# Residual and gate offsets by accumulating DMAs, and more Strassen pairs, in a float32 encoder block

## The chip, the cores and the metric

The kernel runs on one core of a Trainium2 chip. The metric is the device time of one execution in microseconds (us). The engines are TensorE (PE, with PEld for its weight loads and "PE mm" or "PE at" for its work into one or the other set of PSUM banks), VectorE (DVE), ScalarE (ACT), GpSimd (POOL) and SyncE (SP), whose queue starts the weight loads.

## The reference

One encoder layer with 256 tokens of width 2048, in float32:

```
h = LN(alpha*h + 0.5*SwiGLU_1(h))                  # hidden width 5504
h = LN(alpha*h + W_out[sig(g_A)*(A(h) W_oA) + sig(g_B)*(B(h) W_oB)])
h = LN(alpha*h + CrossAttn(h, LN(mem)))            # 4 heads, 256 memory tokens
h = LN(alpha*h + 0.5*SwiGLU_2(h))

swiglu_ffn(x, w_in, w_out): g, u = split(x @ w_in); return (silu(g) * u) @ w_out
g = sigmoid(gates + gate_bias); g_a, g_b = split(g, 2)
```

A is chunked attention with relative-position bias, B is latent attention with a low-rank key and value. The gates `gates` are 4096 columns of one combined projection of h.

## The kernel before

**Products.** All products keep float32 accuracy with operands of a shorter type: every operand is split into a part hi and a rest lo, and hi·hi, hi·lo and lo·hi are summed in PSUM. A weight block of 128 rows and 2048 columns (`raw`, 1 MB) comes by SP's queue; ScalarE casts it to `hi` in two halves (`halves`, L264) and VectorE subtracts to get `lo` (L267). Work goes by pairs of contraction tiles. A plain pair (`mm_pair`, matmuls at L311) has 24 matmuls of 128x512 for four results (two token halves by two column halves).

**Summed pairs.** A pair can also be done in the manner of Strassen (`mm_sums`, matmuls at L366) with 21 matmuls. For it VectorE adds blocks of the weights (`weight_sums`, L248 once on 1024 columns and L250 twice on 512), subtracts a lo of only 1536 columns, and the sums are split as well: ScalarE casts them to X2 in two halves, VectorE subtracts to X3 (L267, 2048 columns). X2 and X3 (`SUM_HOME`) are there once. The activations need a matching form (`forms_step`, `sum_forms`: L321 and four L325 on VectorE, a split by L255 on ScalarE and L256 on VectorE), which is kept at a home that the tables `SUMS_...` name. Of each summed pair part of the results goes to four further PSUM banks (`qs`), which `shared` (L676 on) combines at the end of a group: two copies on ScalarE, four additions on VectorE (L681 to L684). They are added to what the other pairs made in their own banks (`ps`).

**Groups.** `pair_group` (L640 on) lays out the pairs of a group of results in an order, and `at` says which are summed. There are eight pairs in a group of 16 contraction tiles. An FFN runs in two halves of its hidden width (24 and 19 tiles). Each has first its input groups of eight pairs, whose end is the gated product (L725 to L728), then its output. Half 0 has two output groups g0 and g1 of 12 pairs with pairs 3, 5, 7, 9 summed, in the order 0 to 11 (`out_pair`). Half 1 has one of 10 pairs with 3, 5 and 7 summed, and another kind of group (`out_proj`). At the end of `out_pair` the shared results are added to the residual h by VectorE, four operations on 128x512 with the factor ALPHA in the first half (L629) and without in the second (L631); then `finish` (L754) adds each token's and column half's own PSUM bank to h. The cross attention's output product `w_xo` uses `out_pair`, too.

**Gates.** Four groups n of 1024 columns (L917 to L927): `product` adds shared results and PSUM banks to H{n} (L921), adds the bias (L923), which four DMAs on POOL's queue have spread over the partitions of X1 (L912), and takes the sigmoid on ScalarE. Groups 0 and 1 have four summed pairs in the order `ORDER_GATE`, 2 and 3 have three. Then comes the group `w_lat`.

**Order.** `weave` puts steps between the pairs of a group by position; `add` gives a step a priority. Within that a scheduler orders each engine's instructions by times of its own, so a row may move where the code doesn't say so. Buffers: three `raw`, two `hi` and `lo`, six small tiles `w2` (shown as `w`), and in PSUM four banks `mm` and four `at`, between which groups alternate.

Of the kernel before, what the change touches and what calls it, by code (L numbers as in the profile page):

```python
# [14 lines left out]
ALU = mybir.AluOpType  # L15
# [3 lines left out]
P = 128  # L19
S = 256  # L20
D = 2048
KT = D // P
# [5 lines left out]
SUMS_IN = {2: ("X0", 0), 4: ("X0", 1), 6: None}  # L28
AT_FIRST = 4, 6
SUMS_OUT = ({3: ("X1", 0), 5: ("X1", 1), 7: ("X0", 0), 9: ("X0", 1)},  # L30
            {3: ("X1", 0), 5: ("X1", 1), 7: ("X0", 0)})
SUMS_GATE, AT_GATE = {**SUMS_IN, 5: ("F", 0)}, ((2, 4, 5, 6), (2, 4, 5, 6), (2, 4, 6), (2, 4, 6))
ORDER_GATE = (0, 2, 1, 4, 5, 3, 6, 7)
SUMS_YB = {4: ("T0", 0), 6: ("T0", 1), 2: None}
AT_YB = (2, 4, 6), (4, 6)
SUMS_XQ = {4: ("H5", 0), 6: ("H5", 1), 2: None}
# [5 lines left out]
SUM_HOME = ("X2", "X3"),  # L42
# [5 lines left out]
ALPHA = 2.0 ** 0.25  # L48
# [53 lines left out]
class Kernel:  # L102
# [451 lines left out]
    def ffn(self, tag, xT, st, first=None, steps=None, late=None, before=None, tags=None):  # L554


        t = self.t
        f0 = bank = 0
        turn = None
        fx = {}  # L560
        for half, nf in enumerate(F_SPLIT):
            hid, fh, homes = Act([]), {}, SUMS_OUT[half]
            end = half == len(F_SPLIT) - 1
            form = lambda c, fh=fh, homes=homes, hid=hid: self.forms_step(fh, homes, c, lambda: hid)
            for g in range(-(-nf // 4)):
# [12 lines left out]
                if turn and n < 4:  # L578
                    turn[5] = turn.pop(6)
                self.weave(main, turn or {}, prio=0)  # L580
                for c, (home, _) in homes.items():
                    if home == "X1" and c // 2 == g - 1:
                        self.add(form(c))
                hidden, turn = self.hidden(ps, bank, g, n, hid, qs)
                self.add(hidden, prio=SOON)
                if before and 2 <= j < 6:
                    self.add(lambda q=j - 2: self.gb_apply(2, self.h, (q,)), prio=LATE)
                if j == 0 and first is not None:
                    for c in set(SUMS_IN) - set(AT_FIRST):
                        self.add(self.forms_step(fx, SUMS_IN, c, xT, False))  # L590
                bank ^= 1
            if end and late:
                self.add(lambda: setattr(self, "cut", True))

            def out(hid=hid):
                x = lambda: hid
                src = [t[tag + "_w_out"][g, :, f0 * 1024:(f0 + nf) * 1024] for g in range(2)]
                self.out_pair(bank, src[0], 0, nf, x, homes, fh, half == 0, st if end else None,
                              SUM_HOME + ("H5",) if end else SUM_HOME)
                if end:  # L600
                    self.out_proj(tag + "_w_out_r", nf, x, False, st, steps, tags, 2, cut=tags is None)
# [17 lines left out]
    def out_pair(self, bank, src, g, nk, x, at, fx, scale, st, sums_in=SUM_HOME):  # L619

        nc, h = self.nc, self.h
        ps, qs = {}, {}

        def shared():
            for (tt, a), s in qs["add"].items():
                c = (2 * g + a) * 512
                hs = h[tt][:, c:c + 512]
                if scale:
                    nc.vector.scalar_tensor_tensor(hs, hs, ALPHA, s, ALU.mult, ALU.add)  # L629
                else:  # L630
                    nc.vector.tensor_tensor(hs, hs, s, ALU.add)  # L631
# [238 lines left out]
    def mixer(self, xT, st, steps):  # L870
        nc, t = self.nc, self.t
# [24 lines left out]
        ps = {}  # L896
# [3 lines left out]
        a, b, c = steps(1)  # L900
        self.weave(first, {0: a, 3: b, 4: c})
        gates, fx = {}, {}
# [4 lines left out]
        bias = {}  # L907

        def load_bias(n):
            if "t" not in bias:  # L910
                bias["t"] = self.block("X1", (P, 2, 1024))
            nc.gpsimd.dma_start(bias["t"][:, n % 2, :], t["gate_row"][n:n + 1, :].to_broadcast([P, 1024]))  # L912

        def gate(n):
            ps, qs = {}, {}

            def product():  # L917
                g = gates[n] = self.block(f"H{n}", (P, 2, 2, 512))
                for tt in range(2):
                    for a in range(2):  # L920
                        nc.vector.tensor_tensor(g[:, tt, a, :], qs["add"][tt, a], ps[tt, a], ALU.add)  # L921
                    v = g[:, tt].rearrange("p a n -> p (a n)")
                    nc.vector.tensor_tensor(v, v, bias["t"][:, n % 2, :], ALU.add)  # L923
                    nc.scalar.activation(v, v, AF.Sigmoid)
                if n < 2:
                    load_bias(n + 2)
            self.pair_group(n % 2, t["w_gate"][n], 512, KT, xT, AT_GATE[n], fx, ps, qs, None, SUM_HOME + ("H5",),  # L927
                            ORDER_GATE if len(AT_GATE[n]) > 3 else None)
# [54 lines left out]
        self.pair_group(0, t["w_lat"][0], 512, KT, xT, SUMS_IN, fx, lps, lqs, None, SUM_HOME + ("H5",))  # L983
        self.add(lat_scale, prio=SOON)
        self.add(lat_planes)

# [225 lines left out]
        for i in range(NA):  # L1212
            side = [[lat_send(0)], [], [lat_join(0)], [lat_join(1)]][2 * i:2 * i + 2] if i < 2 else ([], [])
# [42 lines left out]
        n = B_HEADS - 1  # L1256
# [55 lines left out]
        main = self.collect(lambda: out_a(0))  # L1312
# [4 lines left out]
        side = out_b(0)  # L1317
        last = {}
        main = self.collect(lambda: last.update(out_b(1)))
# [379 lines left out]
def _layout(i):  # L1699
    import numpy as np  # L1700
    a = {k: np.asarray(v) for k, v in i.items()}
    r = {}
# [5 lines left out]
    for f in ("ffn1", "ffn2"):  # L1708
        w = a[f + "_w_in"][0]
        r[f + "_w_in"] = _pairs(  # L1710
            w[:, D_FF:D_FF + NG * 512], w[:, :NG * 512], 512, [AT_FIRST] + [SUMS_IN] * (NG - 1))
        r[f + "_w_in_r"] = _pairs(
            w[:, D_FF + NG * 512:], w[:, NG * 512:D_FF], D_FF - NG * 512, [SUMS_IN])
        w = a[f + "_w_out"][0]
        at = [*SUMS_OUT[0], *(F_SPLIT[0] // 2 + c for c in SUMS_OUT[1])]
        r[f + "_w_out"] = _pairs(*_halves(w), 512, [at, at])
# [60 lines left out]
```

## Time and profile before

| | us |
|---|---|
| runs of the kernel before | 2432.69, 2434.71 (median), 2434.84 |
| the profiled execution | 2432.52 |
| its span | 2430.7 |
| ScalarE busy in it | 1553.2 (64%) |
| POOL busy in it | 35.9 (1%) |
| first FFN, output groups g0 and g1 | 256.63 to 319.19, to 381.9 |
| gate groups 0 to 3 | 729.85, 770.49, 812.16, 853.97, end 895.78 |
| second FFN, output groups g0 and g1 | 1995.23 to 2057.8, to 2120.5 |

The span is that of the profiler's records; the execution's own time lies 1.8 us above it. The granted TensorE clock was 1.00 throughout. In a timeline a row gives the start, the time taken and the line; VectorE's operations overlap a little at their ends, so that the distance between two starts is what one costs its engine. A table by windows gives each engine's busy time in a stretch.

### The profile page before, as it was taken

Reading aid. Unit: us, or ns where it says so; the run is one execution under the profiler, and the core shown is the slowest. Engines: PE = TensorE matmul, PEld = TensorE weight load, DVE = VectorE, ACT = ScalarE, POOL = GpSimd, SP = SyncE. Lnnn points to the kernel's source line nnn. Section 1 sums busy time; section 2 is a strip of 40 time slices with the busy share of each in tenths; the row PEclk is TensorE's granted clock in tenths of the full one; section 3 lists DMA queues with packets and bytes.
Section 4 is the critical chain, followed back from the end, with each engine's and each line's share of the span. In section 5 each row is a group of like instructions: output and inputs, shape, how many; then the busy total and the mean of one; then the engine's idle time right before and its main releaser. Section 6 shows DMA issues by size and latency. Waiting matters only on the chain.

```text
span 2430.7 us, 29702 instructions
## 1 busy us (share of the span) xinstructions
PE 2422.3 (100%) x11280; PEld 2022.8 (83%) x11280; DVE 2130.9 (88%) x2437; ACT 1553.2 (64%) x2022; POOL 35.9 (1%) x81
## 2 busy tenths in 40 slices
PE   9999999999999999999999999999999999999999
PEld 8888888888888888888888888888888888888887
DVE  8999989899889998779788889979879999888997
ACT  6676745666555557878565687765666675556662
POOL 0000000000000001000000000000000000000000
PEclk9999999999999999999999999999999999999999
DMA  7766656667656657776577577655556766666665
GB/s 268 252 212 214 207 200 222 210 201 219 224 176 215 216 195 248 229 210 176 183 246 256 167 241 213 220 181 192 190 199 214 229 221 210 220 207 207 200 220 182
DMA packets 176414, 516.20 MB, mean 212 GB/s; under 512 B 111728, under 2 KB 112496, under 8 KB 121104
## 3 DMA queue, kind: packets, MB, share of 16 engines
q1 hardware_dynamic: 170816, 495.83, 61.6%
q0 software_dynamic: 4592, 17.30, 2.2%
q8 instruction: 88, 1.44, 0.2%
q10 hardware_dynamic: 864, 1.18, 0.1%
q14 instruction: 54, 0.44, 0.1%
HBM read 485.30 MB, written 2.10 MB: 201 GB/s over the span
## 4 chain that ended last, share of the span: by engine, by line
PE 89%; DVE 4%; ACT 3%; DMA 1%; issue 1%; SPq 0%; DVEq 0%; ACTq 0%
PE at L311 24%; PE mm L311 23%; PE at L366 11%; PE mm L366 11%; PE mm L298 10%; PE mm L277 4%; PE mm L279 2%; DVE lo L267 2%; ACT hi L264 1%; PE at L1034 1%; PE at L1505 0%; PE at L277 0%; DMA raw<-w_xv 0%; PE at L1088 0%; ACT H L854 0%
## 5 line engine op out<-in xcount | busy, mean ns | idle before, releaser
L264 ACT CAST hi<-raw 128x1024 fp32r<-128x1024 f32 (+1 forms) x852 | 804.0, 981 | 458.0 <-PE at L311 150.1
L267 DVE TENSOR_TENSOR lo<-raw,hi 128x2048 fp32r<-128x2048 f32 (+1 forms) x427 | 902.0, 2114 | 134.8 <-ACT hi L264 129.0
L311 PE MATMUL mm<-hi,T 128*128 128x512 f32 (+1 forms) x1312 | 307.5, 384 | 0.8 <-DVE v L400 0.7
L311 PEld LDWEIGHTS mm<-hi,T 128*128 128x128 f32 x1312 | 244.5, 188 | 46.9 <-DVE v L400 1.1
L264 ACT CAST X<-H 128x1024 fp32r<-128x1024 f32 (+1 forms) x170 | 174.8, 1035 | 160.9 <-DVE H L248 119.9
L311 PE MATMUL at<-hi,T 128*128 128x512 f32 x1136 | 272.3, 390 | 0.0
L311 PEld LDWEIGHTS at<-hi,T 128*128 128x128 f32 x1136 | 213.3, 188 | 44.5
L267 DVE TENSOR_TENSOR X<-H,X 128x2048 fp32r<-128x2048 f32 (+1 forms) x85 | 191.4, 2252 | 64.7 <-ACT X L264 64.7
L311 PE MATMUL mm<-lo,T 128*128 128x512 f32 (+1 forms) x656 | 158.4, 383 | 0.0
L311 PE MATMUL at<-lo,T 128*128 128x512 f32 x568 | 141.0, 389 | 0.0
L311 PEld LDWEIGHTS mm<-lo,T 128*128 128x128 f32 x656 | 122.3, 188 | 22.4
L311 PE MATMUL at<-hi,H 128*128 128x512 f32 x560 | 133.8, 390 | 0.0
L311 PEld LDWEIGHTS at<-lo,T 128*128 128x128 f32 x568 | 106.7, 188 | 22.1
L311 PEld LDWEIGHTS at<-hi,H 128*128 128x128 f32 x560 | 105.0, 188 | 21.5
L250 DVE TENSOR_TENSOR H<-H,raw 128x512 f32<-128x512 f32 (+1 forms) x170 | 115.4, 679 | 2.2
L311 PE MATMUL mm<-hi,H 128*128 128x512 f32 x480 | 115.5, 392 | 0.1
L311 PEld LDWEIGHTS mm<-hi,H 128*128 128x128 f32 x480 | 89.6, 188 | 18.9 <-DVE w L684 0.5
L248 DVE TENSOR_TENSOR H<-raw 128x1024 f32<-128x1024 f32 (+1 forms) x85 | 102.1, 1201 | 0.6 <-DMA raw<-w_gate 0.4
L366 PE MATMUL mm<-X,X 128*128 128x512 f32 x342 | 91.4, 393 | 0.0
L264 ACT CAST X<-raw 128x1024 fp32r<-128x1024 f32 (+1 forms) x54 | 55.4, 1035 | 47.9 <-DVE raw L250 38.6
L366 PE MATMUL at<-X,X 128*128 128x512 f32 (+1 forms) x315 | 82.6, 386 | 0.7 <-ACT X L264 0.7
L854 ACT COPY w<-w 128x1024 uint16<-128x1024 uint16 (+1 forms) x60 | 75.7, 1275 | 1.4 <-DMA w<-w 1.4
(387 smaller groups left out, 4151.3 us busy)
## 6 DMA issues: line engine op xcount, KB each, us to landing
raw<-ffn_w_in SPq DMA_DIRECT2D x150, 1024.0 KB, 4.9
raw<-ffn_w_out SPq DMA_DIRECT2D x66, 1024.0 KB, 4.9
raw<-w_gate SPq DMA_DIRECT2D x32, 1024.0 KB, 4.8
raw<-ffn_w_out_r SPq DMA_DIRECT2D x16, 1024.0 KB, 4.9
raw<-w_qk SPq DMA_DIRECT2D x16, 1024.0 KB, 5.6
raw<-w_o_b SPq DMA_DIRECT2D x16, 1024.0 KB, 4.8
raw<-w_out SPq DMA_DIRECT2D x16, 1024.0 KB, 5.0
raw<-w_xk SPq DMA_DIRECT2D x16, 1024.0 KB, 5.4
```

The source lines that it names most:

```text
L248: self.nc.vector.tensor_tensor(two[0], two[1], raw[:, :m].unsqueeze(1).to_broadcast([P, 2, m]), ALU.add)
L250: self.nc.vector.tensor_tensor(t[:, a * m:a * m + m], t[:, b * m:b * m + m], raw[:, a * m:a * m + m], ALU.add)
L264: self.last_hi = self.nc.scalar.copy(hi[:, c:d], src[:, c:d])
L267: self.last_lo = self.nc.vector.tensor_tensor(lo[:, :n], src, hi[:, :n].bitcast(F32), ALU.subtract)
L277: self.nc.tensor.matmul(ps, hi[j], x.both(kt), start=(j == 0), stop=False)
L279: self.last_mm = self.nc.tensor.matmul(ps[:, :S], lo[j], x.at(0, kt), start=False, stop=(j == n - 1))
L298: self.last_mm = self.nc.tensor.matmul(ps, x.at(xi, kt)[:, tt * P:(tt + 1) * P], w[wi][:, j * 512 + c:j * 512 + c + m], start=(start and j ...
L311: self.last_mm = self.nc.tensor.matmul(ps[tt, g][:, :n], x.at(xi, kt)[:, tt * P:(tt + 1) * P], w[wi][:, c:c + n], start=first and j + wi + ...
L366: self.last_mm = self.nc.tensor.matmul(bank[:, :m], a[xi], v[wi][:, c * m:(c + 1) * m], start=own and first and wi + xi == 0, stop=own and ...
L854: self.nc.scalar.copy(self.words(u, n).rearrange("p (c k) -> p k c", k=2), self.words(s, n).rearrange("p (k c) -> p k c", k=2))
L1034: nc.tensor.matmul(ps[:, c0:c0 + nk], q[:, tt * P:(tt + 1) * P], k[:, :nk], start=(j == 0), stop=(j == len(parts) - 1))
```

## The change

- The shared results of `out_pair` are added to h by DMAs with an accumulating addition on POOL's queue (four of 128x512 in each of the seven calls) in place of four VectorE operations. Where ALPHA is wanted, ScalarE multiplies h by it earlier, at position 2 of the group (`scaled`).
- The gate's bias is added by accumulating DMAs, from the row in memory straight to H{n}; the four loads to X1 and the VectorE additions go. The sigmoid stands in a step of its own at position 3 of the next group.
- Gate groups 2 and 3 get the fourth summed pair, whose form is there already.
- The output groups g0 and g1 of half 0 in both FFNs get a fifth summed pair (1, its form at "F"), with the order `ORDER_OUT`: summed pairs at positions 1, 3, 5, 7 and 9.

```diff
-SUMS_GATE, AT_GATE = {**SUMS_IN, 5: ("F", 0)}, ((2, 4, 5, 6), (2, 4, 5, 6), (2, 4, 6), (2, 4, 6))
+SUMS_GATE, AT_GATE = {**SUMS_IN, 5: ("F", 0)}, ((2, 4, 5, 6), (2, 4, 5, 6), (2, 4, 5, 6), (2, 4, 5, 6))
+OUT_MORE, ORDER_OUT = {1: ("F", 1)}, (0, 3, 2, 5, 4, 7, 6, 9, 8, 1, 10, 11)
...
-                self.out_pair(bank, src[0], 0, nf, x, homes, fh, half == 0, st if end else None,
-                              SUM_HOME + ("H5",) if end else SUM_HOME)
+                self.out_pair(bank, src[0], 0, nf, x, homes if end else {**homes, **OUT_MORE}, fh, half == 0, st if end else None,
+                              SUM_HOME + ("H5",) if end else SUM_HOME, order=None if end else ORDER_OUT)
...
-                    self.out_pair(bank ^ 1, src[1], 1, nf, x, homes, fh, half == 0, None)
+                    self.out_pair(bank ^ 1, src[1], 1, nf, x, {**homes, **OUT_MORE}, fh, True, None, order=ORDER_OUT)
...
             if not end:
+                if "F" in fx:
+                    fh["F"] = fx["F"]
+                side[8] = side.get(8, []) + [self.forms_step(fh, OUT_MORE, 1, lambda hid=hid: hid)]
...
+        def scaled():
+            for tt in range(2):
+                hs = h[tt][:, g * 1024:(g + 1) * 1024]
+                nc.scalar.mul(hs, hs, ALPHA)
 
         def shared():
             for (tt, a), s in qs["add"].items():
                 c = (2 * g + a) * 512
-                hs = h[tt][:, c:c + 512]
-                if scale:
-                    nc.vector.scalar_tensor_tensor(hs, hs, ALPHA, s, ALU.mult, ALU.add)
-                else:
-                    nc.vector.tensor_tensor(hs, hs, s, ALU.add)
+                nc.gpsimd.dma_start(h[tt][:, c:c + 512], s, accum_op=ALU.add)
...
-        self.pair_group(bank, src, 512, nk, x, at, fx, ps, qs, shared, sums_in)
+        main = self.collect(lambda: self.pair_group(bank, src, 512, nk, x, at, fx, ps, qs, shared, sums_in, order))
+        self.weave(main, {2: [scaled]} if scale and at else {}, prio=0)
...
                     v = g[:, tt].rearrange("p a n -> p (a n)")
-                    nc.vector.tensor_tensor(v, v, bias["t"][:, n % 2, :], ALU.add)
+                    nc.gpsimd.dma_start(v, t["gate_row"][n:n + 1, :].to_broadcast([P, 1024]), accum_op=ALU.add)
+
+            def ends():
+                for tt in range(2):
+                    v = gates[n][:, tt].rearrange("p a n -> p (a n)")
                     nc.scalar.activation(v, v, AF.Sigmoid)
...
+            self.weave(main, side, prio=0)
             self.add(product, prio=SOON)
-
-        self.add(lambda: [load_bias(n) for n in range(2)])
+            return {3: [ends]}
+
+        side = {}
         for n in range(4):
-            gate(n)
+            side = gate(n, side)
```

VectorE's order at the start of the first FFN's g0, before; the rows at L726 and L728 are the last gated product of the input group ahead of it, the first L248 is the sum for the first summed pair:

```order
L728 SCALAR_TENSOR_TENSOR w2_298_1987<-w2_297_1986,w2_298_1987 128x512
L726 TENSOR_TENSOR w2_299_1988<-w2_299_1988,at_262_1742 128x512
L267 TENSOR_TENSOR lo_303_2023<-raw_301_2020,hi_302_2022 128x2048
L728 SCALAR_TENSOR_TENSOR w2_300_1989<-w2_299_1988,w2_300_1989 128x512
L267 TENSOR_TENSOR lo_310_2068<-raw_308_2065,hi_309_2067 128x2048
L248 TENSOR_TENSOR raw_312_2074<-raw_311_2072 128x1024
L321 TENSOR_TENSOR w2_331_2187<-H3_247_1648 128x512
L250 TENSOR_TENSOR raw_312_2074<-raw_312_2074,raw_311_2072 128x512
L267 TENSOR_TENSOR lo_314_2103<-raw_311_2072,hi_313_2102 128x1536
L250 TENSOR_TENSOR raw_312_2074<-raw_312_2074,raw_311_2072 128x512
```

The same place with the change (its line numbers are 1 to 6 higher: L249 and L251 are L248 and L250 of before, L268 is L267, L732 and L734 are L726 and L728, L326 is L325):

```order
L734 SCALAR_TENSOR_TENSOR w2_300_1993<-w2_299_1992,w2_300_1993 128x512
L732 TENSOR_TENSOR w2_301_1994<-w2_301_1994,at_262_1742 128x512
L249 TENSOR_TENSOR raw_298_1988<-raw_297_1986 128x1024
L734 SCALAR_TENSOR_TENSOR w2_302_1995<-w2_301_1994,w2_302_1995 128x512
L251 TENSOR_TENSOR raw_298_1988<-raw_298_1988,raw_297_1986 128x512
L268 TENSOR_TENSOR lo_304_2027<-raw_297_1986,hi_303_2026 128x1536
L251 TENSOR_TENSOR raw_298_1988<-raw_298_1988,raw_297_1986 128x512
L322 TENSOR_TENSOR w2_330_2164<-H3_247_1648 128x512
L326 TENSOR_TENSOR w2_331_2165<-w2_330_2164 128x128 x2
L326 TENSOR_TENSOR w2_331_2165<-w2_331_2165,w2_330_2164 128x128
L268 TENSOR_TENSOR X3_306_2032<-raw_298_1988,X2_305_2031 128x2048
L268 TENSOR_TENSOR lo_313_2077<-raw_311_2074,hi_312_2076 128x2048
```

The sum L249 stands ahead of the last gated products and of every lo of the group, in place of behind two plain lo, and X3 comes before the second plain lo.

VectorE's order from the first FFN's g0 to g1, before (L684 is the last of the shared results, L754 is `finish`):

```order
L684 TENSOR_TENSOR w2_363_2410<-w2_361_2408,at_325_2154 128x512
L629 SCALAR_TENSOR_TENSOR h0_101<-h0_101,w2_361_2408 128x512
L629 SCALAR_TENSOR_TENSOR h1_102<-h1_102,w2_362_2409 128x512
L629 SCALAR_TENSOR_TENSOR h1_102<-h1_102,w2_363_2410 128x512
L267 TENSOR_TENSOR lo_366_2448<-raw_364_2445,hi_365_2447 128x2048
L754 TENSOR_TENSOR h0_101<-h0_101,mm_304_2037 128x512
L754 TENSOR_TENSOR h0_101<-h0_101,mm_305_2038 128x512
L267 TENSOR_TENSOR lo_369_2479<-raw_367_2476,hi_368_2478 128x2048
L754 TENSOR_TENSOR h1_102<-h1_102,mm_306_2039 128x512
L754 TENSOR_TENSOR h1_102<-h1_102,mm_307_2040 128x512
L248 TENSOR_TENSOR raw_378_2524<-raw_377_2522 128x1024
```

With the change (L690 is L684, L760 is L754):

```order
L690 TENSOR_TENSOR w2_369_2428<-w2_367_2426,at_319_2090 128x512
L268 TENSOR_TENSOR lo_372_2466<-raw_370_2463,hi_371_2465 128x2048
L249 TENSOR_TENSOR raw_374_2472<-raw_373_2470 128x1024
L760 TENSOR_TENSOR h0_101<-h0_101,mm_307_2046 128x512
L251 TENSOR_TENSOR raw_374_2472<-raw_374_2472,raw_373_2470 128x512
L268 TENSOR_TENSOR lo_376_2501<-raw_373_2470,hi_375_2500 128x1536
L251 TENSOR_TENSOR raw_374_2472<-raw_374_2472,raw_373_2470 128x512
L760 TENSOR_TENSOR h0_101<-h0_101,mm_308_2047 128x512
L760 TENSOR_TENSOR h1_102<-h1_102,mm_309_2048 128x512
L268 TENSOR_TENSOR X3_378_2506<-raw_374_2472,X2_377_2505 128x2048
L760 TENSOR_TENSOR h1_102<-h1_102,mm_310_2049 128x512
```

The four residual additions are gone (three of them in the rows of before), the first summed pair of g1 is prepared between the operations of `finish`, and these stand further apart. On POOL four DMAs for each call of `out_pair` come in.

More of the change, by code (lines that the diff above doesn't have):

```diff
@@ L617, in ffn, with out_pair @@
             f0 += nf
-    def out_pair(self, bank, src, g, nk, x, at, fx, scale, st, sums_in=SUM_HOME):
+    def out_pair(self, bank, src, g, nk, x, at, fx, scale, st, sums_in=SUM_HOME, order=None):
         nc, h = self.nc, self.h
         ps, qs = {}, {}
+        def scaled():
+            for tt in range(2):
+                hs = h[tt][:, g * 1024:(g + 1) * 1024]
+                nc.scalar.mul(hs, hs, ALPHA)
         def shared():
@@ L904, in mixer, with gate @@
         self.weave(second, {1 + i: [self.forms_step(fx, SUMS_GATE, c, xT)] for i, c in enumerate(SUMS_GATE)}, prio=0)
[L907 to L914, printed above, removed]
+        def gate(n, side):
             ps, qs = {}, {}
@@ L922, in product @@
                     v = g[:, tt].rearrange("p a n -> p (a n)")
-                    nc.vector.tensor_tensor(v, v, bias["t"][:, n % 2, :], ALU.add)
+                    nc.gpsimd.dma_start(v, t["gate_row"][n:n + 1, :].to_broadcast([P, 1024]), accum_op=ALU.add)
+            def ends():
+                for tt in range(2):
+                    v = gates[n][:, tt].rearrange("p a n -> p (a n)")
                     nc.scalar.activation(v, v, AF.Sigmoid)
[L925 to L928, printed above, removed]
+            main = self.collect(lambda: self.pair_group(
+                n % 2, t["w_gate"][n], 512, KT, xT, AT_GATE[n], fx, ps, qs, None, SUM_HOME + ("H5",),
+                ORDER_GATE if len(AT_GATE[n]) > 3 else None))
+            self.weave(main, side, prio=0)
             self.add(product, prio=SOON)
-        self.add(lambda: [load_bias(n) for n in range(2)])
+            return {3: [ends]}
+        side = {}
         for n in range(4):
-            gate(n)
+            side = gate(n, side)
         lps, lqs = {}, {}
@@ L981, in lat_join @@
             return fn
-        self.pair_group(0, t["w_lat"][0], 512, KT, xT, SUMS_IN, fx, lps, lqs, None, SUM_HOME + ("H5",))
+        main = self.collect(lambda: self.pair_group(
+            0, t["w_lat"][0], 512, KT, xT, SUMS_IN, fx, lps, lqs, None, SUM_HOME + ("H5",)))
+        self.weave(main, side, prio=0)
         self.add(lat_scale, prio=SOON)
@@ L1715, in _layout @@
         at = [*SUMS_OUT[0], *(F_SPLIT[0] // 2 + c for c in SUMS_OUT[1])]
-        r[f + "_w_out"] = _pairs(*_halves(w), 512, [at, at])
+        r[f + "_w_out"] = _pairs(*_halves(w), 512, [[*at, *OUT_MORE], [*at, *OUT_MORE]])
         r[f + "_w_out_r"] = _tok(w[F_SPLIT[0] * P:, D // 2:])
```

## The prediction

> **What bounds the kernel now.** I read the page first (busy shares, then the chain that ended last), then the table of waits, then the timeline and the table by windows where the change acts.
>
> ```profile
> span 2430.7 us, 29702 instructions
> PE 2422.3 (100%) x11280; PEld 2022.8 (83%) x11280; DVE 2130.9 (88%) x2437; ACT 1553.2 (64%) x2022; POOL 35.9 (1%) x81
> ...
> PE 89%; DVE 4%; ACT 3%; DMA 1%; issue 1%; SPq 0%; DVEq 0%; ACTq 0%
> ```
>
> TensorE (PE) is busy for 2422.3 of 2430.7 us and makes up 89% of the chain. VectorE (DVE) is at 88%: a second engine close behind, and the one that the change loads. The longest waits of PE and of its queue (PE mm) are these:
>
> ```profile
> PE at L493 <- DVE w L470: 1.1, 1, 1.1
> PE at L366 <- ACT X L264: 0.7, 2, 0.5
> PE mm L311 <- DVE v L400: 0.7, 1, 0.7
> ```
>
> With smaller ones below them they come to some 3 us in the whole program, so almost nothing is to be had from removed waits: time falls where matmuls go, and rises where PE newly waits. What a matmul is worth is read in the first FFN's first output group:
>
> ```profile
> 256.63 3.79 PE L311 MATMUL mm<-hi,H 128*128 128x512 f32 x16
> ...
> 262.07 3.79 PE L311 MATMUL mm<-hi,H 128*128 128x512 f32 x16
> ...
> 272.95 0.61 PE L366 MATMUL mm<-hi,H 128*128 128x512 f32 x2
> ...
> 277.71 3.79 PE L311 MATMUL mm<-hi,H 128*128 128x512 f32 x16
> ...
> 283.15 0.62 PE L366 MATMUL mm<-hi,H 128*128 128x512 f32 x2
> ```
>
> The plain pair that starts at 277.71 has 24 matmuls (16 hi, 8 lo) and the next starts at 283.15: 5.44 us. The summed pair from 272.95 to 277.71 has 21 in 4.76 us. Both are 0.2267 us each.
>
> **The change part by part.**
>
> *Six more summed pairs.* Gate groups 2 and 3 get one each, four FFN output groups (half 0 of both FFNs, g0 and g1) one each: 6 × 3 = 18 matmuls, 18 × 0.2267 = **−4.08 us**, 0.17% of the time. That is all that the change can take from PE's work; the rest is what VectorE makes of it.
>
> *What VectorE gets and loses.* Here stands how it runs at that place, and how full it is there:
>
> ```profile
> 257.10 0.68 DVE L725 TENSOR_TENSOR w<-w,at 128x512 f32<-128x512 f32 x1
> ...
> 260.10 2.29 DVE L267 TENSOR_TENSOR lo<-raw,hi 128x2048 fp32r<-128x2048 f32 x1
> 262.30 0.69 DVE L728 SCALAR_TENSOR_TENSOR w<-w,w 128x512 f32<-128x512 f32 x1
> ...
> 265.10 1.22 DVE L248 TENSOR_TENSOR raw<-raw 128x1024 f32<-128x1024 f32 x1
> 266.24 0.69 DVE L321 TENSOR_TENSOR w<-H 128x512 f32<-128x512 f32 x1
> ...
> 267.78 1.76 DVE L267 TENSOR_TENSOR lo<-raw,hi 128x1536 fp32r<-128x1536 f32 x1 [0.25 <-PE mm L311]
> 269.46 0.69 DVE L250 TENSOR_TENSOR raw<-raw,raw 128x512 f32<-128x512 f32 x1
> 270.06 0.49 DVE L325 TENSOR_TENSOR w<-w 128x128 f32<-128x128 f32 x2
> 270.46 0.61 DVE L325 TENSOR_TENSOR w<-w,w 128x128 f32<-128x128 f32 x2
> ...
> 270.18 1.05 ACT L264 CAST X<-raw 128x1024 fp32r<-128x1024 f32 x1 [1.71 <-DVE raw L250]
> ...
> 256.60:319.20 62.60, 62.60 (x278) 51.85 (x277) 58.16 (x58) 38.88 (x45) 0.00 (x0) 1.00 0.64 213
> 319.20:381.90 62.70, 62.70 (x278) 51.98 (x277) 53.29 (x50) 31.74 (x35) 0.00 (x0) 1.00 0.59 201
> 1995.20:2057.80 62.60, 62.60 (x278) 51.85 (x277) 60.80 (x62) 38.85 (x45) 0.00 (x0) 1.00 0.65 218
> ```
>
> By the distance from one start to the next, an operation on 512 columns takes 0.60, the sum on 1024 (L248) 1.14, a lo of 2048 2.20, of 1536 1.67. A pair that becomes summed loses one lo of 2048 and gains L248, two L250, a lo of 1536 and one of X (2048): 1.14 + 1.20 + 1.67 + 2.20 − 2.20 = +4.0 us. Its form of the activations, made once for each FFN beside g0, costs L321 0.60, four L325 1.0 (0.40 and 0.61) and one 512-wide L256 0.60: +2.2. The four residual additions leave: −2.4. So g0 gets +3.8, g1 +1.6. PE's length of such a group falls from 62.56 (8 × 5.44 + 4 × 4.76) to 61.88. In g1 VectorE goes to about 54.9 of 61.9: room enough. In the first FFN's g0 it goes to 62.0 of 61.9, in the second's to 64.6 of 61.9. There it becomes the bound: **this is the step on which the forecast turns.**
>
> *First FFN, g0.* The first sums now stand at position 1, which PE reaches at 262.07, not at position 3. VectorE must first end the last gate operations: from 257.10 five of 0.60 to 260.10, then L248 to 261.24, one more 0.60, L250 to 262.44, the lo of 1536 to 264.11, L250 to 264.71. ScalarE's cast of the second half of X starts 0.12 after such an L250 and takes 1.05 (270.18 behind 269.46 + 0.60): X is there at 265.88. PE has 13 matmuls that don't need it, to 262.07 + 13 × 0.2267 = 265.02, and waits 0.9. X's lo follows behind a part of the next form at 268.1, again late, and VectorE stays without a gap to the last X, so that the lag isn't won back. Bounds: 0 if PE takes matmuls of the next plain pair ahead meanwhile (its queue's order has some of these there), 2.5 if X's lo is waited for in full each time. I take **+1.5**.
>
> *Second FFN, g0.* The same walk from 1996.59 (PE at position 1 from 2000.67), with two operations more between, of the layer norm's gain and bias:
>
> ```profile
> 1996.59 0.68 DVE L725 TENSOR_TENSOR w<-w,at 128x512 f32<-128x512 f32 x1
> ...
> 2000.67 3.79 PE L311 MATMUL mm<-hi,H 128*128 128x512 f32 x16
> ```
>
> lo comes at 2003.6 (PE waits 0.7), the X half another 1.1 late: 1.8 at the start, and 64.6 − 61.9 = 2.7 that VectorE lacks within the group: **+4.5**. Bounds: 0 (all covered by PE's order) and 6 (the first FFN's lag of X's lo on top).
>
> *Residual additions as DMAs on GpSimd's (POOL's) queue.* No row shows an accumulating DMA. It can start at the end of the shared results and has to land before finish (L754) adds PE's sums to the same h.
>
> ```profile
> 313.11 1.89 DVE L629 SCALAR_TENSOR_TENSOR h<-h,w 128x512 f32<-128x512 f32 x3
> ...
> 318.71 1.28 DVE L754 TENSOR_TENSOR h<-h,mm 128x512 f32<-128x512 f32 x2 [1.51 <-PE mm L311]
> ...
> 626.54 1.89 DVE L631 TENSOR_TENSOR h<-h,w 128x512 f32<-128x512 f32 x3
> 637.65 2.27 DVE L267 TENSOR_TENSOR lo<-raw,hi 128x2048 fp32r<-128x2048 f32 x1
> ...
> 1696.20 1.89 DVE L629 SCALAR_TENSOR_TENSOR h<-h,w 128x512 f32<-128x512 f32 x3
> 1704.99 2.27 DVE L267 TENSOR_TENSOR lo<-raw,hi 128x2048 fp32r<-128x2048 f32 x1
> ...
> DMA to landing us min/median/max: 3.3/4.2/8.8
> ...
> L912 POOL DMA_DIRECT2D X<-gate_row x4: 528/532/704, 708.7 to 820.4; - x4
> DMA to landing us min/median/max: 5.4/5.8/6.4
> ```
>
> Nearest rows: the loads w<-gb on the same queue land in 3.3 to 8.8 us (the first of these two rows), the wider X<-gate_row in 5.4 to 6.4; POOL takes about 0.53 to issue one. Four issues from 313.1 are done by 315.2, so they land from 316.9 (the first, at 3.3; the group ends at 319.19) to 324.0 (the last, at 8.8). What queues behind the waiting additions on VectorE is the next pair's lo, then sums, so PE; in the new order of g1 the four additions lie apart between these and PE reaches them late: from 313.1 the landing has about 13 us. At the end of half 1 the next lo behind four additions and the statistics (637.65 now) is wanted at about 645; the slack is some 13 us again (from 626.5, with 5 us of additions and statistics to follow), at w_xo 10.5 (from 1696.2, next lo at 1704.99). Bounds of the landing: 3.3 and twice 8.8 = 17.6 for a transfer that reads two sources; I take about 6 to 9, the rows' own, so **nothing**, and keep the late end as a rival. The scaling by ALPHA, now on ScalarE at position 2 (10 operations of about 1 us), lies beside a 64% busy engine; without that cover each would cost up to 1 us.
>
> *From g0 to g1.* Sums at position 1 also need four PSUM banks 5.4 us into the group, which finish must have read; by its new place they come free at about 8.1 us, against 7.9 wanted: **+0.2** (bounds 0 and 2, one lo of 2.2).
>
> *Gates.* The bias addition leaves VectorE (2 × 1.14 in each group; four loads to X leave too), the sigmoid moves into the next group, where ScalarE is 23 to 25 of 41 us busy.
>
> ```profile
> 814.97 1.22 DVE L923 TENSOR_TENSOR H<-H,X 128x1024 f32<-128x1024 f32 x1
> ...
> 729.85:770.49 40.64, 40.64 (x181) 33.65 (x180) 35.69 (x29) 23.08 (x28) 0.00 (x0) 1.00 0.63 222
> 770.49:812.16 41.67, 41.64 (x181) 33.59 (x180) 38.29 (x31) 25.06 (x29) 0.53 (x1) 1.00 0.57 198
> 812.16:853.97 41.81, 41.81 (x184) 34.18 (x183) 39.16 (x33) 23.74 (x27) 0.53 (x1) 1.00 0.65 227
> 853.97:895.78 41.81, 41.81 (x185) 34.46 (x184) 37.34 (x32) 23.78 (x27) 0.00 (x0) 1.00 0.57 196
> ```
>
> Groups of four sums want 4 × 5.44 + 4 × 4.76 = 40.80, of three 41.48. So the four lose 0, 0.87, 0.33 and 0.33, 1.5 in all, to waits. VectorE has +4.0 − 2.3 in groups 2 and 3, about 40.9 and 39.1 of 40.8: as tight as the group at 770.49 was. Bounds −1.5 and +1.5; I take **−0.3**. The accumulated bias has a group's time to land.
>
> Sum: −4.08 + 1.5 + 4.5 + 0.2 − 0.3 = +1.8 us. The profiled execution took 2432.52 us (1.8 beyond its span), so 2434.3; the median of the runs shown, 2434.71, stands 2.2 above it: **2436.5 us**.
>
> **The rivals.**
> *A: the lag is covered.* Where X is late, PE's order has matmuls of the next plain pair to give; For it: the row of waits at L366 above, 0.7 us, is nearly all that summed pairs cost PE now in the whole program. Against: with VectorE at 64.6 of 61.9 no order helps for long. Then −4.08 − 0.3: 2428.1, so 2430.3; with all of the gates' 1.5 won, 2429.1.
> *B: the accumulating DMAs land late* (the slower side). VectorE stands at finish, with lo and sums behind it, and PE behind these. It decides from a landing of about 13 us (10.5 at w_xo). [...] For it: one issue of 704 ns where others take 528, one landing of 8.8, a VectorE that is 85 to 97% busy in these groups. Against: medians of 532 ns and 4.2 us beside the same VectorE. [...]
> *C: VectorE lags in all four output groups.* The first FFN's g0 costs 4.5 as the second's, and each g1 1 us, since the lag is carried into it with its additions: +3 + 2, so 2441.5. For it: 62.0 of 61.9 in the first. Against: g1 at 55 wins back 7 us.
> *The change not doing what it says* I exclude: the fewer matmuls stand in the new order.
>
> **How the numbers follow.** Forecast 0.55 (own range 2433 to 2439.5), A 0.25, C 0.12, B 0.08. The range leaves out B and the ends of A and C: 2429.8 to 2442. A measurement of this kernel tells some 0.2% (4.9 us) from no change, so "same" is 2429.8 to 2439.6: it holds the forecast and most of A, 0.71; faster is the rest of A with all of the gates' waits won, 0.09; slower B and C, 0.20.
>
> **What would show it.** Right: 18 matmuls fewer in PE's groups; PE idle 2 to 6 us in all in the two g0, ended by ScalarE's casts of X and VectorE's lo; VectorE without a gap in the second FFN's g0; h landing 6 to 9 us after its issue and no wait of VectorE on it; gate groups of 40.8 to 41.2. Wrong: VectorE idle before finish, ended by a DMA on h (B); g0 as long as its matmuls, 61.9 (A); g1 with waits (C); a landing above 13 us.

## The result and the profile after

| | us |
|---|---|
| before, median (4 runs, 2432.69 to 2435.29) | 2434.78 |
| changed, median (4 runs, 2456.3 to 2460.24) | 2459.68 |
| ratio | 1.010, 95% interval 1.0088 to 1.0112 |
| changed, the profiled execution, and its span | 2460.24, 2458.4 |

The change made the kernel 25 us slower; the forecast was 2436.5, the range 2429.8 to 2442.0. First the busy shares from the page of the changed kernel, then its longest waits of PE:

```profile
span 2458.4 us, 29798 instructions
PE 2428.8 (99%) x11262; PEld 2017.6 (82%) x11262; DVE 2134.1 (87%) x2437; ACT 1571.4 (64%) x2046; POOL 65.3 (3%) x113
...
PE at L367 <- ACT X L265: 7.2, 6, 4.6
PE mm L299 <- DVE lo L268: 2.4, 1, 2.4
PE mm L367 <- DVE X L268: 1.9, 4, 0.8
PE mm L367 <- ACT X L265: 1.8, 2, 1.5
PE mm L278 <- ACT hi L265: 1.5, 1, 1.5
PE at L422 <- issue: 1.5, 1, 1.5
PE mm L312 <- DVE w L690: 1.1, 2, 0.8
```

PE has 18 matmuls fewer (11262), as it should, and yet is busy 6.5 us longer: behind two waits matmuls run at a granted clock of 0.50 (last section), and around other waits, too, more time goes than the wait itself (in the second FFN's g0, 1.34 us pass around a wait of 0.61 where two matmuls take 0.45); the waits themselves, some 3 us before, are now 24 us. The first name among them is ScalarE's cast of the sums X, at six places. Where they lie shows in a table by stage. I took the start of the same matmul in both traces (PE's instructions are all there, so they can be counted: three fewer behind each group with a further summed pair), in us:

```
stage                            before   after    more   by the prediction
first FFN, g0                     62.56   63.21   +0.65   +0.8
first FFN, g1                     62.79   63.33   +0.54   -0.6
first FFN, half 1, input groups  197.04  199.18   +2.15    0
first FFN, out_proj               51.38   52.90   +1.51    0
gate groups 0 to 3               165.92  169.76   +3.84   -1.7
w_lat                             41.65   48.76   +7.11    0
cross attention's k, q and v     155.20  160.06   +4.87    0
w_xo_r, behind w_xo               19.49   23.81   +4.32    0
second FFN, g0                    62.56   66.41   +3.85   +3.8
second FFN, g1                    62.79   62.11   -0.68   -0.6
all other                                         -0.5
```

Where the loss stands isn't where the working had put it. In the second FFN's g0, which carried the forecast's largest term, the loss is as worked out; in gates and w_lat, where the working had a gain, 11 us were lost. Here are the timelines at w_lat: first two rows of ScalarE before, then ScalarE, POOL's issues and PE in the changed kernel:

```profile
902.12 1.06 ACT L924 ACTIVATE H<-H 128x1024 f32<-128x1024 f32 x1 [1.07 <-DVE H L923]
906.83 1.05 ACT L264 CAST X<-H 128x1024 fp32r<-128x1024 f32 x1
...
907.68 1.57 ACT L265 CAST hi<-raw 128x1024 fp32r<-128x1024 f32 x2 [1.15 <-PE mm L312]
912.32 1.06 ACT L927 ACTIVATE H<-H 128x1024 f32<-128x1024 f32 x1 [3.06 <-DMA H<-gate_row]
913.28 1.03 ACT L265 CAST X<-H 128x1024 fp32r<-128x1024 f32 x1
918.33 1.06 ACT L927 ACTIVATE H<-H 128x1024 f32<-128x1024 f32 x1 [4.01 <-DMA H<-gate_row]
919.29 1.98 ACT L265 CAST hi<-raw 128x1024 fp32r<-128x1024 f32 x2
921.17 1.04 ACT L265 CAST X<-H 128x1024 fp32r<-128x1024 f32 x1
...
907.04 0.86 POOL L922 DMA_DIRECT2D H<-gate_row  x1 [41.97 <-DVE H L920]
908.23 0.86 POOL L922 DMA_DIRECT2D H<-gate_row  x1 [0.33 <-DVE H L920]
...
916.56 1.07 PE L367 MATMUL at<-X,X 128*128 128x512 f32 x4
922.27 1.22 PE L367 MATMUL at<-X,X 128*128 128x512 f32 x2 [4.64 <-ACT X L265]
```

The two sigmoids of the group before (L927) stand on ScalarE 5 and 10 us after their transfers were issued. ScalarE waits for the landing 3.06 us before the one and 4.01 before the other. Behind the second in its queue stand the casts of the next weight block and of the second half of X (921.17): that half PE stands waiting for, 4.64 us. Before, the second sigmoid (902.12) waited 1.07 us for VectorE, and no wait of PE for such a cast was longer than 0.5 us. The transfer that was to relieve VectorE has put ScalarE, which had a third of its time free, on the critical path.

At the end of w_xo it is VectorE that stands. The first of the four transfers is issued at 1709.82; POOL's issues of the other three and what they do to VectorE and PE:

```profile
1715.23 2.63 POOL L636 DMA_DIRECT2D h<-w  x3 [4.52 <-DVE w L688]
...
1715.58 0.68 DVE L690 TENSOR_TENSOR w<-w,mm 128x512 f32<-128x512 f32 x1
1722.76 0.69 DVE L760 TENSOR_TENSOR h<-h,at 128x512 f32<-128x512 f32 x1 [2.89 <-DMA h<-w]
1724.32 0.69 DVE L760 TENSOR_TENSOR h<-h,at 128x512 f32<-128x512 f32 x1 [0.87 <-DMA h<-w]
1728.35 0.69 DVE L760 TENSOR_TENSOR h<-h,at 128x512 f32<-128x512 f32 x1 [2.14 <-DMA h<-w]
1729.68 2.27 DVE L268 TENSOR_TENSOR lo<-raw,hi 128x2048 fp32r<-128x2048 f32 x1
...
1732.01 1.85 PE L299 MATMUL mm<-lo,X 128*128 128x512 f32 x4 [2.41 <-DVE lo L268]
```

`finish` (L760) waits 2.89, 0.87 and 2.14 us for h; the lo behind it (1729.68), on which PE's next matmuls wait 2.41 us, starts 13.4 us after the end of the shared results (L690, 1716.26); before, it was 8.8 us (1704.99 and 1696.20). The last transfer, issued at 1716.55, landed 11.8 us later.

### The profile page after: what moved, and what is told of

It reads as the page before. It is cut to its first block, busy times and chain, and to the rows that moved or that the text cites. A ratio compares the mean times of both kernels' runs of the same rounds, so it can differ in the third digit from the quotient of the medians.

```text
span 2458.4 us, 29798 instructions
## 1 busy us (share of the span) xinstructions
PE 2428.8 (99%) x11262; PEld 2017.6 (82%) x11262; DVE 2134.1 (87%) x2437; ACT 1571.4 (64%) x2046; POOL 65.3 (3%) x113
## 5 line engine op out<-in xcount | busy, mean ns | idle before, releaser
L268 DVE TENSOR_TENSOR lo<-raw,hi 128x2048 fp32r<-128x2048 f32 (+1 forms) x427 | 898.5, 2105 | 146.6 <-ACT hi L265 141.5
L268 DVE TENSOR_TENSOR X<-H,X 128x2048 fp32r<-128x2048 f32 (+1 forms) x87 | 196.0, 2252 | 64.1 <-ACT X L265 64.1
L312 PE MATMUL at<-hi,H 128*128 128x512 f32 x528 | 125.8, 389 | 0.0
L251 DVE TENSOR_TENSOR H<-H,raw 128x512 f32<-128x512 f32 (+1 forms) x174 | 118.0, 678 | 2.1
L312 PEld LDWEIGHTS at<-hi,H 128*128 128x128 f32 x528 | 98.9, 188 | 20.3
L312 PE MATMUL mm<-hi,H 128*128 128x512 f32 x448 | 110.2, 392 | 0.4 <-DVE w L690 0.4
L249 DVE TENSOR_TENSOR H<-raw 128x1024 f32<-128x1024 f32 (+1 forms) x87 | 104.5, 1201 | 5.1 <-DMA raw<-ffn_w_in 4.4
L312 PEld LDWEIGHTS mm<-hi,H 128*128 128x128 f32 x448 | 83.3, 188 | 18.7 <-DVE w L690 0.8
L265 ACT CAST X<-raw 128x1024 fp32r<-128x1024 f32 (+1 forms) x62 | 63.7, 1038 | 51.0 <-DVE raw L251 37.7
L268 DVE TENSOR_TENSOR X<-raw,X 128x2048 fp32r<-128x2048 f32 (+1 forms) x31 | 69.8, 2255 | 12.7 <-ACT X L265 12.6
```

The lines of the kernel that those rows point to most:

```text
L249: self.nc.vector.tensor_tensor(two[0], two[1], raw[:, :m].unsqueeze(1).to_broadcast([P, 2, m]), ALU.add)
L251: self.nc.vector.tensor_tensor(t[:, a * m:a * m + m], t[:, b * m:b * m + m], raw[:, a * m:a * m + m], ALU.add)
L265: self.last_hi = self.nc.scalar.copy(hi[:, c:d], src[:, c:d])
L268: self.last_lo = self.nc.vector.tensor_tensor(lo[:, :n], src, hi[:, :n].bitcast(F32), ALU.subtract)
L312: self.last_mm = self.nc.tensor.matmul(ps[tt, g][:, :n], x.at(xi, kt)[:, tt * P:(tt + 1) * P], w[wi][:, c:c + n], start=first and j + wi + ...
```

## The experiments

Each of the kernels was timed beside the kernel before; the stage figures are of one profiled execution each, by the same count of matmuls. Two theories stood against each other: that an engine stands at a landing, and with it what is queued behind (1), and that the further pairs overload VectorE (2). A third is contention: that the transfers slow the weight loads (3).

How much a stage differs from one profile to the next can be read, too. Ahead of the gates and behind w_lat, the kernels with late sigmoids and with the gate's bias as before have every engine's instructions in the order of the changed kernel. In the changed kernel and these two, in this order, w_xo_r has +4.32, +4.57 and +4.73, the first g0 +0.65, +0.64 and +0.69, the second g0 +3.85, +3.63 and +3.55: these agree. Half 1's input groups have +2.15, +0.30 and +3.53, out_proj +1.51, −0.17 and −0.17, the first g1 +0.54, +0.13 and +0.65. So in the latter stages one profile doesn't tell what an edit is worth.

**Late sigmoids.** The changed kernel with:

```diff
-                    nc.scalar.activation(v, v, AF.Sigmoid)
+                    with self.tc.issue_after(self.next_hi.ins):
+                        nc.scalar.activation(v, v, AF.Sigmoid)
...
-            return {3: [ends]}
+            return {5: [ends]}
```

(The first hunk puts the sigmoid behind `next_hi`, the last cast begun, in ScalarE's order.)

> The changed kernel (2459.7 us) with one edit: each gate's two sigmoids stand on ScalarE behind the last cast of the next group's last summed pair, some 25 us after the bias transfers are issued, in place of 4 to 6 us after. Theory 1 (ScalarE stands at the sigmoid until the accumulating transfer has landed, 15.5 us in all, and the casts of the sums X queue behind it): gates and w_lat, 218.5 us in the changed kernel, lose 8 to 12 us; 2448 to 2452 us. Theory 2 (the fourth summed pair loads VectorE too much): at most 2 us less, 2457 to 2460. Theory 3 (the accumulating transfers take bandwidth from the weight loads): no change, 2459 to 2461.

Measured 2445.38 us (ratio to before 1.0044, 1.0029 to 1.0059), 14.3 less than the changed kernel, more than expected. w_lat comes to 41.64 (−0.01 against before), gate groups 1 to 3 to −0.67, −0.38 and −0.20: 12.2 of the 14.3 us lie in these stages. Theory 1 holds, and the fourth summed pair costs nothing where ScalarE doesn't stand; theories 2 and 3 had 2457 or more. No row of ScalarE waits for a bias transfer any more, though the transfers land as late as before (the view of L922's transfers, duration in ns and landing in us; first the changed kernel, then this one):

```profile
L922 POOL DMA_DIRECT2D H<-gate_row x8: 863/866/871, 776.3 to 908.2; - x8
  ACT H L927: 15.5, 6
DMA to landing us min/median/max: 5.1/6.1/10.1
```

```profile
L922 POOL DMA_DIRECT2D H<-gate_row x8: 863/863/868, 772.3 to 899.1; - x8
DMA to landing us min/median/max: 5.0/6.1/9.8
```

**The gate's bias as before, with the fourth pairs.** The hunks of the gates undone, but for `AT_GATE`.

> The changed kernel with the gate's bias as before (loads to X1, an addition on VectorE, the sigmoid right behind it), but all four groups with four summed pairs. Theory 1: the waits of ScalarE go, gates and w_lat come to some 206 to 208 us, 2447 to 2449 us in all. Theory 2: VectorE has 2.3 us more in each group and is the bound, so nothing is won or up to 5 us lost: 2459 to 2465. Theory 3: as theory 1, but the weight loads there land earlier too.

Measured 2451.47 us (1.0070, 1.0055 to 1.0085): less than the changed kernel, but more than theory 1 had. w_lat is at +0.66, gate groups 2 and 3, which got the fourth pair, at +2.36 and +1.97. So theory 2 has its share: with the bias additions on VectorE (2.3 us more in each group; it is busy 40.7 of 43.5 us in group 2) a fourth pair costs 2 us and more instead of saving 0.7. Taking the bias off VectorE was right for PE; only where ScalarE took it up was wrong.

**The bias transfers without the fourth pairs.** The kernel before with the gate hunks alone and `AT_GATE` as before.

> The kernel before with the gate's bias by accumulating transfers and the sigmoid at position 3 of the next group, three summed pairs in gate groups 2 and 3 as before, everything else as before. Theory 1: ScalarE stands at the sigmoid before the same casts: w_lat +6 to +8 us, the other gates +0 to +2 each: 2442 to 2446 us against 2435. If the fourth summed pair is needed for the loss: w_lat +0 to +1, 2435.

Measured 2442.68 us (1.0031, 1.0020 to 1.0042), within what was expected; the places are others. Group 2 has +6.32, group 1 +1.65, w_lat +1.61: the loss falls on whichever group has a sigmoid just ahead of a cast that PE wants. ScalarE's waits in this part, and the longest of them:

```profile
ACT H L922 <- DMA H<-gate_row: 22.1, 7, 6.4
```

**The residual additions on VectorE again.** The changed kernel with `shared` and the factor ALPHA as before:

```diff
-                nc.gpsimd.dma_start(h[tt][:, c:c + 512], s, accum_op=ALU.add)
+                hs = h[tt][:, c:c + 512]
+                if scale:
+                    nc.vector.scalar_tensor_tensor(hs, hs, ALPHA, s, ALU.mult, ALU.add)
+                else:
+                    nc.vector.tensor_tensor(hs, hs, s, ALU.add)
```

> The changed kernel with the residual additions back on VectorE in all seven calls. Theory 1 (VectorE stands at the end of a group until the transfers on h have landed): the 4.3 us at w_xo and the 1.5 us of half 1 come back, and VectorE's 2.4 us more in each output group cost 2 to 4 us, above all in the second FFN's g0: 2456 to 2459 us. Theory 3 (28 transfers of 256 KB disturb the weight loads): 2450 or less. A rival that the transfers are free: 2462 to 2464.

Measured 2453.53 us (1.0079, 1.0064 to 1.0094): 6.2 less. w_xo_r goes from +4.32 to 0.00, the first g1 from +0.54 to −0.68, out_proj from +1.51 to +0.05, the input groups of half 1 from +2.15 to −0.36; VectorE's 2.4 us more cost 1.2 and 1.4 us in the two g0. The time came out lower than expected; g1 and half 1's input groups, which I hadn't counted, are part of it, as far as single profiles tell. At the start of half 1 a landing is awaited not only by `finish` but by a form, which takes a small tile `w` that a transfer still reads (VectorE's timeline in the changed kernel):

```profile
384.08 0.50 DVE L326 TENSOR_TENSOR w<-w 128x128 f32<-128x128 f32 x2 [1.56 <-DMA h<-w]
```

VectorE stood 1.56 us there, until the transfer that reads the tile had landed: not only h but the source, too, wasn't free before the landing here.

**The transfers alone.** The kernel before with the residual hunks alone.

> The kernel before with the residual additions as accumulating DMAs alone (ALPHA on ScalarE, 28 transfers); pairs and gates as before. Theory 1 (VectorE stands at the end of a group until the transfers have landed): the output product of the cross attention costs 2.5 to 4.5 us, the end of the first FFN's half 1 0.5 to 1.5, the other output groups 0 to 2: 2437 to 2441 us against 2434.1 of before. Rival (VectorE's 2.4 us less in each group are worth something to PE): 2434 or less. Rival (the accumulating transfers slow the weight loads everywhere): a loss in the output groups themselves, 2445 or more.

Measured 2437.18 us (1.0012, 1.0003 to 1.0021; 10 runs from 2434.47 to 2442.65): 2.0 us slower, at the low end of theory 1. In the profiled execution, one of the slower at 2441.05, the loss stands behind w_xo (+2.36 and +3.74 in the next stage) and in half 1 (+1.25, +0.53); in g0 and g1 themselves it is 0.00, so neither the relief of VectorE nor contention moves PE there.

**Without the fifth pairs.** The changed kernel with `homes` and the order as before in all output groups.

> The changed kernel without the fifth summed pair and its order in the FFN output groups (residual and gate edits stay). By the walk on VectorE the fifth pair costs 4.5 us in the second FFN's g0 and 1.3 in the first's and saves 2.7 us of matmuls in four groups: without it 2456 to 2458 us. If VectorE's load isn't the cause of the 66.4 us of the second FFN's g0, the matmuls come back for nothing: 2462.

Measured 2449.90 us (1.0066, 1.0049 to 1.0083): 9.8 less, where 2 to 4 were expected. All four output groups come to +0.00 against before, so they give back 4.4 us, where the walk on VectorE had some 3; 1.2 of the 4.4 are the first g1's, which VectorE's load doesn't cost: with the residual additions back on VectorE it was gone. The rest stands in half 1's input groups (−2.2), which differ by as much between profiles, and in the cross attention (−4.5), with which the fifth pairs have nothing to do; that part is told below.

**The fifth pairs later.** The changed kernel with another order:

```diff
-OUT_MORE, ORDER_OUT = {1: ("F", 1)}, (0, 3, 2, 5, 4, 7, 6, 9, 8, 1, 10, 11)
+OUT_MORE, ORDER_OUT = {1: ("F", 1)}, (0, 2, 4, 3, 6, 5, 8, 7, 10, 9, 1, 11)
```

> The changed kernel (2459.7 us) with the five summed pairs of the output groups at positions 3, 5, 7, 9 and 10 in place of 1, 3, 5, 7 and 9. In the second FFN's g0, 66.4 us in the changed kernel and 62.6 before, it tells the two halves of VectorE's lag apart: if the start (1.8 us by the walk) is the sums' early place alone, g0 comes to 64 to 65 us; if VectorE's work in the group (64.6 us) is the whole bound, it stays at 66 to 67; if neither, 62. The first FFN's g0 would come to 61.9 to 62.5.

One run: 2468.63 us. The second FFN's g0 comes to 64.37 (+1.81 in place of +3.85), the first's to 62.73 (+0.17): the start's lag, 1.8 us by the walk, is the sums' early place, and 2 us are gone with it. What is left, 2.5 us beyond the 61.88 of its matmuls, fits the 2.7 by which VectorE's work exceeds the group, but no run takes that work away alone. The later place costs more elsewhere: the shared results come nearer to the group's end, h lands up to 12.4 us after, the second FFN's g1 has +2.93, and the input groups behind the output groups of the two FFNs have +6.41 and +3.74.

**Plain transfers in place of accumulating ones.** `accum_op` left out in both lines; all engines' orders are the same, row by row.

> The changed kernel with plain transfers in place of accumulating ones (the residual and the gate's sums are overwritten by what should be added to them); every engine's instructions stand in the same order. It measures the price of the addition in the transfer by itself. If the addition makes the landing late: the second bias transfer of a gate lands after 5.5 to 7 us in place of 9.8 to 10.1, h<-w after 4 to 6 in place of 6.2 to 11.8, w_lat comes down from +7.1 to +1 to 3 us, w_xo's end from +4.3 to +1 to 2: 2446 to 2452 us. If it is the queue (one transfer behind the other, whatever they do): landings and time as in the changed kernel, 2456 to 2460.

Measured 2441.11 us (1.0026, 1.0016 to 1.0035): of the 25 us lost, some 18 are the addition in the transfer (24.9 us above the kernel before with it, 6.9 without). The time is below the 2446 to 2452 us expected. The scaling by ALPHA on ScalarE is still in this kernel, so it isn't what cost time behind w_xo. The two views of the transfers on h, of the changed kernel and of this one:

```profile
L636 POOL DMA_DIRECT2D h<-w x28: 853/888/1334, 306.6 to 2391.8; - x28
  DVE h L760: 7.2, 6
  DVE w L326: 1.6, 1
DMA to landing us min/median/max: 4.3/7.4/11.8
```

```profile
L636 POOL DMA_DIRECT2D h<-w x28: 536/536/709, 307.6 to 2372.9; - x28
  DVE h L760: 0.9, 1
DMA to landing us min/median/max: 3.7/5.6/7.5
```

POOL issues one in 536 ns in place of 888, it lands after 5.6 us in place of 7.4 (at most 7.5 in place of 11.8), and VectorE hardly waits. The bias transfers likewise:

```profile
L922 POOL DMA_DIRECT2D H<-gate_row x8: 527/527/533, 773.4 to 901.2; - x8
  ACT H L927: 1.9, 2
DMA to landing us min/median/max: 3.8/4.7/6.0
```

The second of a pair lands 5.2 to 6.0 us after its issue, in place of 7.0 to 10.1. w_lat comes to +2.02, w_xo_r to 0.00, out_proj to −0.16, half 1's input groups to +0.43. The queue's line of the two pages shows the same bytes in more packets (packets, MB, share of 16 engines; the changed kernel first):

```profile
q0 software_dynamic: 9200, 26.74, 4.6%
```

```profile
q0 software_dynamic: 7408, 26.74, 3.3%
```

**Two versions put together from it.** The first is the kernel before with the gate part alone and late sigmoids; the second has the fifth pair in g1 too, its form made in g1, and g0 as before.

> The kernel before with the gate part of the change alone, and its sigmoids behind the last cast of the next group's last summed pair (as in the run with late sigmoids): bias by accumulating DMAs, four summed pairs in all four groups. Theory 1: gates and w_lat lose 1.2 us against before and nothing else changes: 2432 to 2434 us. Theory 3 (contention): 2436 or more.

Measured 2434.49 us, ratio 1.0000 (0.9992 to 1.0009): no difference. w_lat and the gates come to −0.3 in all; group 2 has +0.55 where the run with late sigmoids had −0.38.

> As the run before it, and the fifth summed pair in the two output groups g1 alone (form made in g1, residual additions on VectorE, order of g0 as before). By the walk VectorE has 53.3 + 4.0 + 2.2 = 59.5 us in a group of 61.9, so g1 keeps its 0.68 us each: 2.6 us less than before in all, 2430.5 to 2433 us. Rival (sums at position 1 wait for banks or VectorE there too): g1 loses up to 1 us each, 2433 to 2436.

Measured 2434.75 us, 0.9999 (0.9990 to 1.0008): no difference. Each g1 saves its 0.68 us, as the walk had it, but the time lies above the 2430.5 to 2433 expected: 1.4 us in one profile are less than the 2 us or so that these runs tell apart, and no version was faster than the kernel before.

## Why the prediction was wrong

- **Six summed pairs, −4.08 us**: right. 18 matmuls went, and where no engine stands (the second FFN's g1, and g1 in the last version) a group is shorter by exactly 0.68 us.
- **The two g0, +1.5 and +4.5**: right in mechanism and size. Net of 0.68 they had +0.8 and +3.8, measured +0.65 and +3.85; without the fifth pair +0.00; with later sums the start's 2 us go. Here are PE and VectorE at the second FFN's g0, where the walk had put 0.7 on lo and 1.1 on X:

```profile
2027.92 0.50 PE L367 MATMUL mm<-lo,H 128*128 128x512 f32 x1 [0.61 <-DVE lo L268]
2029.60 0.73 PE L367 MATMUL at<-X,X 128*128 128x512 f32 x2 [0.71 <-ACT X L265]
...
2026.12 1.75 DVE L268 TENSOR_TENSOR lo<-raw,hi 128x1536 fp32r<-128x1536 f32 x1
2029.60 2.28 DVE L268 TENSOR_TENSOR X<-raw,X 128x2048 fp32r<-128x2048 f32 x1
...
2019.42:2085.84 66.42, 64.05 (x275) 50.37 (x274) 64.93 (x68) 43.19 (x49) 3.51 (x4) 1.00 0.69 217
```

 They are 0.61 and 0.71, and the rest comes at the sums of positions 7 and later, with VectorE busy 64.9 us in the group (64.6 by the working). The working names two operations of the layer norm ahead of these sums, but its times leave them out (1996.59 to 2003.6 is the first FFN's 257.10 to 264.11); in the run the two stood behind the sums, at 2028.39, so the times held.
- **"The accumulated bias has a group's time to land", −0.3**: the step that failed first, 12.2 us. The code puts the sigmoid at position 3 of the next group, and I read that as time to spare. The time to spare ended at the first instruction that stood behind the wait in ScalarE's queue and that somebody needed. That was the cast of the second half of X (921.17), for which PE stood from 917.63 on. The transfer landed only just before the sigmoid at 918.33, and the sigmoid and two casts of weights still stood ahead of that cast. The prediction asked what is queued behind VectorE's additions, and not what is queued behind ScalarE's sigmoid. The order of ScalarE's rows would have shown it.
- **"About 6 to 9, the rows' own", so nothing for the residual transfers**: mis-sized. Rows of plain loads were taken for a transfer that adds; the last of four landed after 11.6 us at g1 and 11.8 at w_xo, 12 us after the shared results there, beyond the 10.5 that the text itself gives as the point, and it cost 4.32 at w_xo and 0.8 to 1.3 in the first g1 (three profiles); out_proj and half 1's input groups had 1.5 and 2.2 more in the profiled execution, but differ by that much between profiles. With the additions back on VectorE the kernel took 6.2 us less. The wait on a source tile wasn't thought of.
- **Rival B**: the right kind of loss (a landing that is awaited) at 0.08. What it names in its favour, a slow issue beside a busy VectorE, isn't what made the landings late: plain transfers at the same places beside the same VectorE were issued in 0.54 to 0.71 us and landed after 7.5 us at most. With the addition, the issues took 0.85 to 1.33 us and the landings up to 11.8. That the measured time came out on B's side, the slower one, is luck: B has nothing on the gates and w_lat, where 11 us were lost.
- **Gates' fourth pair**: right that it pays only without the bias on VectorE (with it, +2.0 to +2.4 in place of a gain); with late sigmoids the three later groups gave 1.25 us against 1.66 expected.
- **Open**: the stages of the cross attention had +4.9 us in the changed kernel's profile. In other kernels with the same code there they had +0.4 to +3.5, and three of these, with every engine's instructions in the changed kernel's order there, had +1.9, +2.2 and +2.4: half of the 4.9 differs by the profile. In the changed kernel one transpose that SP issues ahead of a weight load took 2.41 us to issue (1.23 before), and the load's cast came late for PE (1.5 us, the row at L278). Whether the change has a part in the rest stays open.

## What to carry to other kernels

Work that was handed from a busy engine to a transfer came back as a wait on the engine that reads the sum (15.5 us on ScalarE at the sigmoids, 7.2 on VectorE at `finish`): before such a step, list what stands behind that reader in its queue, and whether it can stand further back than the landing. An accumulating transfer isn't to be priced by plain loads: here it landed after up to 11.8 us where plain ones at the same places took up to 7.5. And an engine with a third of its time free (ScalarE, busy 64%) had no slack at the place where the bound engine waited for it (PE, 4.64 us).

## What the runs showed of the hardware that was not expected

- **The addition in the transfer is dear.** With all else in the same order: issue 888 against 536 ns, median landing 7.4 against 5.6 us, for two bias transfers in a row 10.1 against 6.0 at most.
- **Two waits of PE cost more than their length.** The windows (length; busy us by engine, the granted clock and the DMAs' share behind) of the wait in w_lat and what follows, then of the one behind w_xo, then of one in gate group 3:

```profile
917.60:922.20 4.60, 0.03 (x1) 0.00 (x0) 0.90 (x1) 3.87 (x5) 0.00 (x0) 0.75 0.49 203
922.20:925.60 3.40, 3.33 (x8) 2.65 (x9) 3.40 (x2) 1.48 (x3) 0.00 (x0) 0.50 0.27 63
925.60:929.00 3.40, 3.40 (x14) 2.72 (x13) 3.37 (x4) 0.29 (x1) 0.00 (x0) 0.83 0.61 251
...
1729.70:1732.00 2.30, 0.00 (x0) 0.00 (x0) 2.30 (x3) 2.30 (x3) 0.00 (x0) 1.00 0.00 0
1732.00:1735.40 3.40, 3.39 (x9) 2.64 (x10) 3.40 (x2) 0.07 (x1) 0.00 (x0) 0.54 0.72 236
...
868.80:870.30 1.50, 0.03 (x1) 0.00 (x0) 0.20 (x2) 1.50 (x3) 0.00 (x0) 1.00 1.04 186
870.30:873.70 3.40, 3.40 (x15) 2.82 (x16) 3.40 (x2) 2.38 (x3) 0.00 (x0) 1.00 0.98 393
```

 The first wait, of 4.64 us, has a mean clock of 0.75 within it: the clock fell to 0.50 some 2.3 us after PE had stopped (919.9, and 917.63) and stayed there for some 6.8 us in all, to 926.75. The 4.5 us of these that lie behind the wait cost 2.3 us on top of it. At the second, of 2.41 us, it fell to 0.50 some 2.7 us after PE had stopped, just behind the wait, and stayed there for some 3.4 us (1732.3 to 1735.7), which costs 1.7; after a wait of 1.48 us it stays at 1.00. How long PE stands doesn't decide alone: behind PE's last matmul the clock stayed at 1.00 for the 4.5 us to the end of the span in the changed kernel (from 2453.9), and fell to 0.50 after 2.8 us in the kernel before (2426.3 to 2429.1), the only time that it left 1.00 there. What else decides, these runs don't show.
